# A float32 transformer step on one core: weight preparation in other steps, sample rows transposed later, one more Strassen pair in place of two plain gates

## The chip, the core and the metric

One core of a Trainium2 chip runs one launch. The metric is the device time in microseconds of that launch (us below). The engines of the core are named as in the profile: PE multiplies matrices (PEld is its weight load), DVE is the vector engine, ACT the activation engine, POOL the general engine, and SP issues the transfers (DMAs).

## The reference

One decoder layer over 1024 prompt rows and 8 x 4 sample rows, 1056 rows (tokens) in all, of width 1024, in float32:

```python
h = LN1(alpha*x + 0.5*SwiGLU_a(x))          # w1, w3: 1024x2816, w2: 2816x1024
z = h @ w_in + b_in                         # 42 column blocks of 128
A = dilated_window_attention(q, k, v of z)  # blocks 0..17
B = u * (tril(W_s) LN(v) + b)               # blocks 18..25 after gelu
h = LN2(alpha*h + (sigmoid(gA)*(A@w_oa) + sigmoid(gB)*(B@w_ob)) @ w_out)
y = LN3(alpha*h + 0.5*SwiGLU_b(h))          # gA: blocks 26..33, gB: blocks 34..41
```

It also returns the attention's key and value windows, for prompt and sample, and the normalised rows of the gating branch.

## The kernel before

**Arithmetic.** Every float32 operand is split in two (`split`, L252: a rounded high part copied by ACT, a low part subtracted by DVE), and every product is three matmuls of 128x128 by 128x264 (`mm3`, L238): high by high, high by low, low by high. The 1056 tokens are four chunks of C = 264. All matmuls of the weights stand on L242.

**Plain blocks and pairs.** A plain block of 128 output columns takes 8 row blocks x 3 matmuls in each of four chunks (`gate8`, L988, for the gates: 24 matmuls a chunk, evicted by ACT in L994 and sent to scratch). Two blocks together can go through a seven-product Strassen scheme (Winograd's form): the weights make seven combinations of halves (`prep`, L370), the activations make seven (`spread`, L329, in `self.T`), and each of the seven products takes 4 row blocks x 2 token halves x 3 matmuls (`product`, L416). The order is 1, 2, 6, 7, 5, 4, 3. `hidden` (L442) does so for one block of w1 beside one of w3, in both feed-forward parts (21 blocks in the first, 20 in the second), and `pair` (L1017) for two blocks of w_in. After each product come its evictions from the accumulators (L1034 on ACT, L1043 on DVE in a pair), traced in `urgent()`, and then a call of `between`. There are three sets of accumulator banks; the set `one` serves products 1, 6, 5 and 3, so a product waits until the evictions of the one before it in the same set are done.

**Preparation.** `prep` is a generator that `begin(f + 1)` starts at the head of block f and that `between` moves on by one step per product. In the kernel before its steps are: transfers of both weight blocks ab and cd (L376, L377) and the split of ab; the sums s12 (L386, L387); the split of s12 and half of s34 (L392); the rest of s34 (L394) and the split of cd's half; the split of s34. The sums run on POOL, or on DVE for the first pair and the first two feed-forward blocks. Two raw buffers (tag R), eight weight buffers (W) and two for the sums (Q) go round.

**Order.** The program is written in trace order, and a compiler pass with a simulated time line orders each engine's instructions; an engine then works strictly in that order. `urgent` raises the priority of evictions by 300. `fenced` (L154) makes what is traced inside it stand behind the last urgent instruction of DVE, of ACT, and behind the last weight transfer of SP. Background work stands in three queues, `bg`, `slow` and `mid`, and `tick(n, m)` takes n steps of `bg`, m of `slow`, 3 of `mid`, all fenced. `prep`'s steps are not fenced.

**The stage of w_in** (`widen`, L1087). Three gates are computed chunk by chunk behind the first layer norm; then three more (`NLEAD = 6`), each with its own weights in W. Their eight ticks take steps of `spread` too. During the last of them pair 0 is prepared. Then 13 pairs: nine of q, k and v, two each of v and u of the gating branch. After a pair of q, k and v, `sample_rows` (L1370) pauses for 4 steps of `bg` (three per product), then PE transposes the sample rows of the pair's two outputs (L1375). After every third such pair `sample` (L1388), the sample rows' attention, joins `slow`: it streams keys and values (kv) in 256 KB pieces that DVE multiplies and reduces (L1421, L1422, L1432, L1437). Behind the pairs `mix` does ten plain gates, the prompt's attention and the two output projections.

Of the kernel before, what the change touches and what calls it, by code (L numbers as in the profile page):

```python
# [16 lines left out]
ALU = mybir.AluOpType  # L17
# [13 lines left out]
FB = 2816 // P  # L31
# [28 lines left out]
REST = 3  # L60
GAP = 4
AFTER = 100
LATE = 16
MID = 3
HOP = (4, 1, 4)
# [3 lines left out]
FENCED = (mybir.EngineType.DVE, mybir.EngineType.Activation, mybir.EngineType.SP)  # L69
QKV = [s * 6 + 2 * g + hp for hp, g in HPG for s in range(3)]  # L70
GATES = [*range(34, 42), *range(26, 34)]
NLEAD = 6
NTAIL = 10
LAST = 3
EARLY = 6
BESIDE = {2: 13, 4: 14, 5: 15}
CHUNKED = 3
SPLIT = [*QKV, 22, 23, 24, 25, 18, 19, 20, 21, *GATES[NLEAD : 16 - NTAIL]]
DENSE = GATES[:NLEAD] + GATES[16 - NTAIL :]
# [4 lines left out]
class Trunk:  # L84
# [285 lines left out]
    def prep(self, src, f, H, engine):  # L370

        nc = self.nc
        lo, hi, n = slice(0, H), slice(H, 2 * H), 2 * H
        with self.tc.high_priority(offset=URGENT):
            ab, cd = self.R([P, D])[:, :n], self.R([P, D])[:, :n]
            nc.sync.dma_start(ab, src[1])  # L376
            dma = nc.sync.dma_start(cd, src[0])  # L377
        self.copy_state(dma, 2)
        tt = engine.tensor_tensor
        ah, al = self.W([P, D]), self.W([P, D])  # L380
        self.split(ah[:, :n], al[:, :n], ab)
        if f == LASTW2:
            h34, l34 = self.held([P, D], F32R), self.held([P, D], F32R)
        yield
        s12 = self.Q([P, D])
        tt(s12[:, lo], cd[:, lo], cd[:, hi], op=ALU.add)  # L386
        tt(s12[:, hi], s12[:, lo], ab[:, lo], op=ALU.subtract)  # L387
        yield
        s34 = self.Q([P, D])
        h12, l12 = self.W([P, D]), self.W([P, D])  # L390
        self.split(h12[:, :n], l12[:, :n], s12[:, :n])
        tt(s34[:, lo], ab[:, lo], cd[:, lo], op=ALU.subtract)  # L392
        yield
        tt(s34[:, hi], ab[:, hi], s12[:, hi], op=ALU.subtract)  # L394
        part = lambda h, l, o=0: [((h, l), o + k * P) for k in range(H // P)]
        if n == D:
            dd = self.S([P, D], F32R)
            self.split(dd[:, lo], dd[:, hi], cd[:, hi])
            p4 = part(dd[:, lo], dd[:, hi])
        else:  # L400
            p4 = []
            for h, l, w in ((ah, al, D - n), (h12, l12, H - (D - n))):
                o = H + len(p4) * P
                self.split(h[:, n : n + w], l[:, n : n + w], cd[:, o : o + w])
                p4 += part(h, l, n)[: w // P]
        yield
        if f != LASTW2:
            h34, l34 = self.S([P, D], F32R), self.S([P, D], F32R)
        self.split(h34[:, :n], l34[:, :n], s34[:, :n])
        self.L[f] = {  # L410
            1: part(ah, al), 2: part(ah, al, H), 5: part(h12, l12), 6: part(h12, l12, H),
            7: part(h34, l34), 3: part(h34, l34, H), 4: p4,
        }
        yield

    def product(self, t, p, f, first):  # L416
        while any(p not in t for t in self.T):
# [257 lines left out]
    def ffn(self, w13, w2p, w2, i, mode, resid):  # L675
        nc, preps = self.nc, {}
        plain = PLAIN[: 1 if i == 0 else 2]
        blocks = [f for f in range(FB) if f not in plain] + [FB + g for g in range(NG * (KB // 2))]
        after = dict(zip(blocks, blocks[1:]))

        def begin(f):
            if f < FB:
                preps[f] = self.prep(w13[f], f, KH * P, nc.gpsimd if f > 2 else nc.vector)
            else:
                preps[f] = self.prep(w2p[f - FB], f, HP, nc.vector)
            next(preps[f])

        if i == 0:
            self.lns = {}
            self.T, self.L = ({}, {}), {}  # L690
            units = self.lead_in(w13)
            self.new_x(1)
            self.consts()
            s0, s1 = (self.spread(j, self.Y, self.A, self.nc.vector) for j in range(2))
            begin(1)
            with self.tc.high_priority(offset=URGENT):
                for k in range(2):
                    self.load_x(self.nc.sync, 3, k, 0, KH)
            for c, work in enumerate((((2,), s0, s0, 1), ((3,), s0, 1, 1), (s1, s1, s1, 1), (1, s0))):
                self.hidden8(units, 0, c)  # L700
                for x in work:
                    if isinstance(x, tuple):
                        self.new_x(*x)
                    else:
                        next(preps[x] if x == 1 else x, None)
            self.bg.extend((s0, s1))
        else:
            lead, s1 = self.early
            lns, self.lns = self.lns, {}
            self.drain(lns[NC - 2])  # L710
            self.step(self.bg, 1)
            begin(1)
            for c in range(NC):
                self.drain(lns.pop(c))
                if c == NC - 1:
                    self.bg.append(s1)
                    self.step(self.bg, 2)
                for f, u in zip(plain, lead):
                    self.hidden8(u, f, c)
                    if c:  # L720
                        with self.chained():
                            next(preps[1], None)
            lead = self.early = None
        self.sqs = {}
        self.Y = self.A = None
        loads = deque(self.load_sums(resid))
        total = len(loads)

        def ready(f):
            for _ in preps.pop(f):  # L730
                pass
            if f in after:
                begin(after[f])

        def between(f, bg, slow=0):
            if after.get(f) in preps:
                next(preps[after[f]], None)
            self.tick(bg, slow)

        def load(n):  # L740

            with self.tc.high_priority(offset=URGENT):
                while loads and total - len(loads) < n:
                    loads.popleft()()

        for f in blocks[: FB - len(plain)]:
            ready(f)
            if f == FB - 1:
                load(2)
            count = iter(range(1, 8))  # L750

            def step():
                between(f, STEPS["strassen"])
                if f == FB - 1:
                    load(min(HEAD, 2 + 4 * next(count)))

            self.hidden(f, step)
            del self.L[f]
        self.T = ({}, {})
        self.normed = [None] * NC  # L760
        self.out(w2, i, mode, ready, between, load)
# [63 lines left out]
    def out(self, w2, i, mode, ready, between, load):  # L825
# [101 lines left out]
        for c in range(NC):  # L927
            early = 6 if c == 0 else 0
            if mode != "out":
                self.hold_normed(c)  # L930
                if c == 2:
                    self.early = [self.unit(self.a["wzp"][n], slot=True, ahead=AFTER) for n in range(CHUNKED)]
            for n in range(KB):
# [14 lines left out]
    def tables(self):  # L948
# [8 lines left out]
        for g in range(3):  # L957
            nc.sync.dma_start(oh[g], a["ohP"][:, g])
        yield from self.pause(LATE)
        for g in range(3):  # L960
# [126 lines left out]
    def widen(self):  # L1087
# [13 lines left out]
        preps = {}  # L1101
# [14 lines left out]
        units = Y = None  # L1116
        for n in range(CHUNKED, NLEAD):
            w = self.unit(a["wzp"][n])
            if n == NLEAD - 1:
                begin(0)  # L1120
            for c in (1, 3, 0, 2):
                self.gate8(w, DENSE[n], c, AF.Sigmoid, STEPS["lead"], 1)
                if n == NLEAD - 1:
                    next(preps[0], None)
        self.A = None
        for f in range(NZ):
            for _ in preps.pop(f):
                pass
            if f < NZ - 1:
                begin(f + 1)  # L1130

            def between():
                if f + 1 in preps:
                    next(preps[f + 1], None)
                self.tick(STEPS["strassen"], 1)

            self.pair(f, between)
            del self.L[f]
# [230 lines left out]

    def sample_rows(self, *blocks):  # L1370
        nc, a = self.nc, self.a
        yield from self.pause(4)
        p = self.ax_tile()[:NS, : 2 * P].rearrange("p (s x) -> p s x", s=2)
        for x, (_, t) in enumerate(blocks):
            nc.tensor.transpose(p[:, x], t[:, NP:], self.ident)  # L1375
        st = self.M([NS, 2, P])
        nc.vector.tensor_copy(st, p)
        for x, (nb, _) in enumerate(blocks):
            s, g, hp = nb // 6, (nb % 6) // 2, nb % 2
            L = GROUPS[g][0]  # L1380
            nc.sync.dma_start(
                self.sD[g, s, 2 * hp : 2 * hp + 2].rearrange("h t e -> t h e"),
                st[:, x].rearrange("t (h e) -> t h e", h=2),
            )
            if s:
                nc.sync.dma_start(a[f"ws{g}"][:, L - 4 :, 256 * (s - 1) + P * hp : 256 * (s - 1) + P * hp + P], st[:, x])
# [522 lines left out]
```

## Time and profile before

| | us |
|---|---|
| median of 3 runs | 2153.39 |
| lowest and highest of them | 2152.51, 2158.67 |
| the profiled execution | 2154.51 |
| its span, first to last instruction | 2152.5 |

In the profile's terms the stages are: the lead-in (0 to 40), the first w1/w3 stage (40 to 461), its w2 stage (to 655), the layer norm with the three chunked gates (to about 751), three plain gates (to 789), 13 pairs (to about 1059), `mix` with its layer norm (to about 1495), the second w1/w3 stage (to about 1904), its w2 stage and the last layer norm.

How to read the lines: a row of the windows gives for a stretch its length, each engine's busy us with the number of its instructions, the granted clock of PE as a share of full speed, the busy share of the transfer engines and their GB/s. A row of the timeline gives start, length, engine, line, operation, output<-input, shape and count of neighbours merged into it, and in brackets the idle time before it and what ended that. A row of the chain of waits gives start, length and what the chain went through.

### The profile page before, as it was taken

How to read it: one execution, taken by the hardware profiler on the slowest of the kernel's cores; microseconds unless marked ns; L12 is line 12 of the kernel's file. 1: busy time of each engine (PE TensorE's matmuls, PEld its weight loads, DVE VectorE, ACT ScalarE, POOL GpSimd, SP SyncE). 2: the span in 40 equal slices, each digit the busy share in tenths (PEclk: the TensorE clock that was granted, in tenths of full speed). 3: DMA queues.
4: the chain of work that ended last, by engine and by line, in shares of the span. 5: the costliest groups of instructions: out<-in, count | busy, mean ns of one | idle time of the engine just before them, and what ended most of it. 6: DMA issues, size and time to landing. Idle time of an engine off the chain costs nothing.

```text
span 2152.5 us, 43254 instructions
## 1 busy us (share of the span) xinstructions
PE 2122.6 (99%) x17307; PEld 2085.6 (97%) x17307; DVE 1549.5 (72%) x2727; ACT 889.4 (41%) x1680; POOL 317.1 (15%) x249
## 2 busy tenths in 40 slices
PE   9999999999999999999999999999999999999997
PEld 8999999999999999999988889999999999999997
DVE  8877767747789834777767758787667777657887
ACT  5444444422124634333476544164444444421224
POOL 0432322200000011323000000000323323100000
PEclk9999999999999999999999999999999999999998
DMA  4444555598885335676865765423454554596852
GB/s 155 145 140 170 183 166 168 189 338 315 327 325 176 130 103 177 201 231 198 296 211 187 223 190 177 154 110 110 144 174 156 183 173 153 194 408 267 311 186 81
DMA packets 168377, 426.51 MB, mean 198 GB/s; under 512 B 24352, under 2 KB 59792, under 8 KB 165488
## 3 DMA queue, kind: packets, MB, share of 16 engines
q1 hardware_dynamic: 167744, 423.21, 56.4%
q8 instruction: 135, 2.21, 0.4%
q10 hardware_dynamic: 432, 0.54, 0.1%
q14 instruction: 66, 0.54, 0.1%
HBM read 304.31 MB, written 165.57 MB: 218 GB/s over the span
## 4 chain that ended last, share of the span: by engine, by line
PE 89%; DVE 4%; DMA 4%; POOL 1%; issue 1%; ACT 0%; SPq 0%; ACTq 0%; DVEq 0%; POOLq 0%
PE ax L242 46%; PE mm L242 39%; DMA R<-wz 1%; PE ax L1206 1%; DMA M<-kv 1%; DMA S<-cD 1%; PE ax L1255 1%; PE ax L1232 1%; DVE W L254 1%; DMA S<-hD 0%; DVE S L632 0%; POOL Q L392 0%; POOL Q L387 0%; DVE S L254 0%; PE ax L621 0%
## 5 line engine op out<-in xcount | busy, mean ns | idle before, releaser
L242 PE MATMUL mm<-S,W 128*128 128x264 f32 x5400 | 713.6, 287 | 8.0 <-ACT S L253 2.3
L242 PE MATMUL ax<-S,W 128*128 128x264 f32 x5400 | 708.6, 285 | 1.3 <-ACT S L1034 1.1
L242 PEld LDWEIGHTS mm<-S,W 128*128 128x128 f32 x5400 | 677.1, 189 | 21.0 <-issue 7.0
L242 PEld LDWEIGHTS ax<-S,W 128*128 128x128 f32 x5400 | 678.5, 189 | 4.0 <-ACT S L1034 2.4
L242 PE MATMUL ax<-S,S 128*128 128x264 f32 x3240 | 475.9, 284 | 1.0 <-ACT S L1034 0.5
L242 PEld LDWEIGHTS ax<-S,S 128*128 128x128 f32 x3240 | 427.7, 188 | 1.7 <-DVE S L1043 0.9
L242 PE MATMUL mm<-S,S 128*128 128x264 f32 x2280 | 359.4, 286 | 2.6 <-DVE S L925 2.6
L242 PEld LDWEIGHTS mm<-S,S 128*128 128x128 f32 x2280 | 311.0, 189 | 3.9 <-issue 2.9
L253 ACT CAST W<-R 128x256 fp32r<-128x256 f32 (+2 forms) x175 | 130.6, 764 | 307.5 <-PE mm L242 139.9
L386 POOL TENSOR_TENSOR Q<-R 128x512 f32<-128x512 f32 x49 | 68.1, 1390 | 800.8 <-DMA R<-w13a 198.2
L254 DVE TENSOR_TENSOR W<-R,W 128x256 fp32r<-128x256 f32 (+2 forms) x175 | 154.6, 887 | 23.3 <-ACT W L253 21.7
L253 ACT CAST W<-Q 128x1024 fp32r<-128x1024 f32 (+1 forms) x78 | 76.8, 984 | 217.2 <-POOL Q L387 88.1
L820 DVE SCALAR_TENSOR_TENSOR S<-ax,S 128x264 f32<-128x264 f32 x240 | 99.7, 429 | 66.1 <-PE ax L242 65.7
L462 DVE TENSOR_TENSOR S<-ax,M 128x264 f32<-128x264 f32 x82 | 32.6, 433 | 144.7 <-PE ax L242 144.7
L254 DVE TENSOR_TENSOR S<-Q,S 128x1024 fp32r<-128x1024 f32 (+1 forms) x78 | 113.6, 1456 | 5.5 <-ACT S L253 5.4
L110 POOL CAST S<-ones 128x1 fp32r<-128x1 f32 x36 | 12.5, 355 | 675.7 <-PE ax L242 226.0
L254 DVE TENSOR_TENSOR W<-Q,W 128x1024 fp32r<-128x1024 f32 (+1 forms) x78 | 90.6, 1161 | 29.6 <-ACT W L253 29.6
L253 ACT CAST S<-Q 128x1024 fp32r<-128x1024 f32 (+1 forms) x78 | 76.7, 984 | 68.4 <-PE ax L242 49.8
L254 DVE TENSOR_TENSOR S<-S,M 128x528 fp32r<-128x528 f32 x72 | 84.6, 1175 | 2.5 <-ACT M L253 0.7
L253 ACT CAST S<-R 128x512 fp32r<-128x512 f32 (+1 forms) x62 | 42.0, 677 | 98.9 <-DMA sumsA<-S 40.6
L387 POOL TENSOR_TENSOR Q<-Q,R 128x512 f32<-128x512 f32 x49 | 81.0, 1653 | 2.7
L394 POOL TENSOR_TENSOR Q<-R,Q 128x512 f32<-128x512 f32 x49 | 79.7, 1627 | 1.2
(209 smaller groups left out, 2042.5 us busy)
## 6 DMA issues: line engine op xcount, KB each, us to landing
ws<-st SPq DMA_DIRECT2D x144, 256.0 KB
S<-sumsA SPq DMA_DIRECT2D x63, 528.0 KB
S<-sumsB SPq DMA_DIRECT2D x63, 528.0 KB
M<-kv SPq DMA_DIRECT2D x96, 256.0 KB
sumsA<-M SPq DMA_DIRECT2D x90, 264.0 KB
sumsB<-M SPq DMA_DIRECT2D x90, 264.0 KB
R<-w13b SPq DMA_DIRECT2D x44, 512.0 KB
R<-w13a SPq DMA_DIRECT2D x42, 512.0 KB
```

The lines of the kernel that those rows point to most:

```text
L110: self.nc.gpsimd.tensor_copy(t[:, 0, :1] if len(shape) == 3 else t[:, :1], self.ones[:, :1])
L242: mm = lambda a, b, s, e: nc.tensor.matmul(o, a[:, cc], b, start=s, stop=e, skip_group_check=True)
L253: a = self.nc.scalar.copy(hi, src)
L254: b = self.nc.vector.tensor_tensor(lo, src, hi.bitcast(F32), op=ALU.subtract)
L386: tt(s12[:, lo], cd[:, lo], cd[:, hi], op=ALU.add)
L387: tt(s12[:, hi], s12[:, lo], ab[:, lo], op=ALU.subtract)
L394: tt(s34[:, hi], ab[:, hi], s12[:, hi], op=ALU.subtract)
L462: go(one, 5, False, lambda x: tt(h[:, x, 1], one[x], p7[:, x], op=ALU.add))
L820: nc.vector.scalar_tensor_tensor(y(x, r, e), bank[x], HALF, y(x, r, e), op0=ALU.mult, op1=ALU.add)
L1206: m = nc.tensor.matmul(pS[h][:, r, :nk], q[e, i * P : (i + 1) * P], k[e, k0 : k0 + nk], start=True, stop=True)
L1232: nc.tensor.transpose(pT[r][:, h, o], s[:, r, h, o], self.ident)
L1255: nc.tensor.matmul(pv[0][e, (i % 4) * P : (i % 4 + 1) * P], V[:, i - (nb - 1) + b, e], sT[:, r, h, b * P : b * P + P], start=b == 0, stop= ...
```

## The change

1. `prep` for w1/w3 and for w_in (`f < FB`; the w2 blocks have higher numbers) has the same number of steps with other contents: transfers; split of ab and s12; half of s34; split of s12, the rest of s34 and the split of cd's half; split of s34. 
2. These steps go through the new `advance`, which fences them, but for the last w1/w3 block, the w2 blocks and pair 0.
3. `sample_rows` pauses for 8 steps in place of 4.
4. Gates 38 and 39 are no longer plain: `NLEAD` is 4, and they are a fourteenth pair, the last, with a sigmoid. Pair 0 is prepared during the one plain gate that is left, with one more call of its generator at that gate's last chunk.

```diff
+ROWS = 8
-NLEAD = 6
+NLEAD = 4
-BESIDE = {2: 13, 4: 14, 5: 15}
+BESIDE = {2: 11, 4: 12, 5: 13}
@@ prep
         tt = engine.tensor_tensor
+        late = f < FB
+        if late:
+            yield
         ah, al = self.W([P, D]), self.W([P, D])
         self.split(ah[:, :n], al[:, :n], ab)
         if f == LASTW2:
             h34, l34 = self.held([P, D], F32R), self.held([P, D], F32R)
-        yield
+        if not late:
+            yield
         s12 = self.Q([P, D])
         tt(s12[:, lo], cd[:, lo], cd[:, hi], op=ALU.add)
         tt(s12[:, hi], s12[:, lo], ab[:, lo], op=ALU.subtract)
         yield
         s34 = self.Q([P, D])
+        if late:
+            tt(s34[:, lo], ab[:, lo], cd[:, lo], op=ALU.subtract)
+            yield
         h12, l12 = self.W([P, D]), self.W([P, D])
         self.split(h12[:, :n], l12[:, :n], s12[:, :n])
-        tt(s34[:, lo], ab[:, lo], cd[:, lo], op=ALU.subtract)
-        yield
+        if not late:
+            tt(s34[:, lo], ab[:, lo], cd[:, lo], op=ALU.subtract)
+            yield
         tt(s34[:, hi], ab[:, hi], s12[:, hi], op=ALU.subtract)
...
+    def advance(self, gen, fenced=True):
+        if gen is not None:
+            with self.fenced() if fenced else ExitStack():
+                next(gen, None)
@@ ffn
         def between(f, bg, slow=0):
-            if after.get(f) in preps:
-                next(preps[after[f]], None)
+            self.advance(preps.get(after.get(f)), f < FB - 1)
             self.tick(bg, slow)
@@ widen
                 self.gate8(w, DENSE[n], c, AF.Sigmoid, STEPS["lead"], 1)
                 if n == NLEAD - 1:
-                    next(preps[0], None)
+                    for _ in range(2 if c == 2 else 1):
+                        next(preps[0], None)
...
             def between():
-                if f + 1 in preps:
-                    next(preps[f + 1], None)
+                self.advance(preps.get(f + 1))
                 self.tick(STEPS["strassen"], 1)
@@ sample_rows
-        yield from self.pause(4)
+        yield from self.pause(ROWS)
```

## The prediction

> **What bounds the kernel now.** I read the head of the page first, then the busy time by stage (windows), then the chain of waits, then the timelines of PE, ACT and DVE where the windows show PE short of work.
>
> ```profile
> span 2152.5 us, 43254 instructions
> PE 2122.6 (99%) x17307; PEld 2085.6 (97%) x17307; DVE 1549.5 (72%) x2727; ACT 889.4 (41%) x1680; POOL 317.1 (15%) x249
> ```
> ```profile
> 40.00:461.00 421.00, 421.00 (x3458) 421.00 (x3457) 304.49 (x411) 182.33 (x320) 119.87 (x76) 1.00 0.51 170
> ...
> 655.00:790.00 135.00, 132.13 (x1067) 131.18 (x1066) 94.96 (x142) 73.73 (x125) 7.26 (x8) 0.99 0.37 125
> 790.00:893.00 103.00, 103.00 (x849) 102.70 (x847) 59.02 (x94) 40.55 (x79) 27.42 (x20) 1.00 0.52 175
> 893.00:1003.00 110.00, 106.69 (x850) 104.55 (x849) 84.09 (x148) 43.17 (x86) 29.94 (x20) 0.98 0.66 214
> 1003.00:1058.00 55.00, 54.48 (x448) 54.27 (x447) 40.09 (x71) 23.43 (x44) 5.72 (x4) 1.00 0.74 250
> ...
> 1095.00:1300.00 205.00, 200.40 (x1692) 179.98 (x1691) 134.15 (x402) 119.59 (x319) 4.13 (x11) 1.00 0.60 193
> ...
> 1495.00:1904.00 409.00, 409.00 (x3366) 409.00 (x3365) 285.92 (x400) 172.74 (x305) 111.22 (x72) 1.00 0.52 180
> ```
>
> The first figures of a row are its length and PE's busy time. PE sets the time: 99% of the span. In both w1/w3 stages it has no idle time at all (421.00 of 421, 409.00 of 409), so an easier preparation has nothing to give there. Of the pairs, the stretch from 893 to 1003 stands out: 850 matmuls in 110 us, where 790 to 893 did 849 in 103. Only two things can therefore shorten this kernel by this edit: fewer matmuls, and that stretch.
>
> **Part 1, the work (a fourteenth pair for two gates).** Two gates are 2 x 4 chunks x 24 = 192 matmuls; a pair is 7 products x 24 = 168.
>
> ```profile
> 734.17 1.61 PE L242 MATMUL ax<-S,W 128*128 128x264 f32 x12
> ...
> 751.45 37.96 PE L242 MATMUL mm<-S,W 128*128 128x264 f32 x312
> ...
> 789.25 3.09 PE L242 MATMUL ax<-S,W 128*128 128x264 f32 x24
> ```
> ```profile
> 800.94 5.96 PE ax L242 x49
> ...
> 883.59 5.96 PE ax L242 x49
> ...
> 1014.50 5.93 PE ax L242 x49
> ...
> 1034.88 5.96 PE ax L242 x49
> ```
>
> The first three rows are PE's timeline (the first is used in part 3): 312 matmuls from 751.45 to 789.25, that is 37.80 / 312 = 0.1212 us each, so two gates are 192 x 0.1212 = 23.26 us. The other four are the chain at the same product of four pairs. A pair without sample rows, which the gate pair is, takes 1034.88 - 1014.50 = 20.38 us. The sum of part 1 is 23.26 - 20.38 = 2.9 us saved.
>
> **Part 2, the stretch 893 to 1003.** The same rows measure its loss. Four pairs from 800.94 to 883.59 take 82.65, or 20.66 each with their sample rows; the six from 883.59 to 1014.50 take 130.91, against 6 x 20.66 = 123.96. So 6.95 us are lost. Where?
>
> ```profile
> 913.96 0.39 PE L1375 MATMUL ax<-ident,S 128*32 128x128 f32 x2 [0.53 <-ACT S L1034]
> 914.59 3.44 PE L242 MATMUL ax<-S,W 128*128 128x264 f32 x24 [0.23 <-ACT S L1034]
> ...
> 927.61 3.60 PE L242 MATMUL ax<-S,S 128*128 128x264 f32 x24 [0.38 <-DVE S L1043]
> ...
> 933.46 3.07 PE L242 MATMUL mm<-S,W 128*128 128x264 f32 x24
> 937.75 0.40 PE L1375 MATMUL ax<-ident,S 128*32 128x128 f32 x2 [1.21 <-ACT S L1034]
> 938.38 4.98 PE L242 MATMUL ax<-S,W 128*128 128x264 f32 x24 [0.23 <-ACT S L1034]
> ...
> 1002.68 3.20 PE L242 MATMUL ax<-S,W 128*128 128x264 f32 x24 [0.58 <-ACT S L1034]
> ```
> ```profile
> 911.75 1.05 ACT L253 CAST W<-Q 128x1024 fp32r<-128x1024 f32 x1 [4.89 <-POOL Q L387]
> 912.71 1.20 ACT L1034 ACTIVATE S<-ax,cols 128x264 f32<-128x264 f32 x3
> ...
> 935.26 1.05 ACT L253 CAST W<-Q 128x1024 fp32r<-128x1024 f32 x1 [13.15 <-POOL Q L387]
> 936.22 1.47 ACT L1034 ACTIVATE S<-ax,qb 128x256 f32<-128x256 f32 x5
> ...
> 1000.46 1.05 ACT L253 CAST W<-Q 128x1024 fp32r<-128x1024 f32 x1 [5.55 <-POOL Q L387]
> 1001.41 1.59 ACT L1034 ACTIVATE S<-ax,cols 128x264 f32<-128x264 f32 x4
> ```
> ```profile
> 940.00:945.00 5.00, 5.00 (x31) 5.00 (x31) 3.19 (x7) 3.16 (x5) 0.00 (x0) 0.70 0.68 227
> ```
>
> PE's five waits on ACT add up to 0.53 + 0.23 + 1.21 + 0.23 + 0.58 = 2.78 us. Behind them 24 matmuls took 3.44, 4.98 and 3.20 in place of 3.09 (row at 789.25): 0.35 + 1.89 + 0.11 = 2.35 more. The 1.89 are the clock: 940 to 945 has a granted clock of 0.70. That makes 5.1 us. The wait on DVE costs 0.38 + (3.60 - 3.09) = 0.9, and 0.9 stay unexplained.
>
> ACT's timeline names the cause. Each time ACT stood in its order at the split of s12 (L253, W<-Q), waiting for POOL, and the evictions that PE needed (L1034) were queued right behind it. The transposes of the sample rows (L1375) wait for the last of those evictions.
>
> The change takes exactly this away. The split of s12 moves from the step after product 2 to the step after product 6, and, fenced, it must stand behind that product's evictions. In the case at 935.26 product 2 was over at 936.5 (row at 933.46), product 6 would have been at 939.5, and POOL's sums were done at 935.26: ACT would not have waited. The transposes also move one product later (8 pauses at 3 per product, against 4), another 2.9 us for the evictions. What is late next on ACT is the split of ab, now behind product 1's evictions, which waits for a transfer; the eviction behind it is product 6's, two products later, so it has 5.8 us. So I take all 5.1 as saved, and leave the DVE wait and the rest. The ends: nothing saved, if another instruction blocks ACT or DVE as long; 6.95 at most.
>
> A rule of the Trainium skill (TensorE: Matmul & The Clock Gate, section "HAM oscillation — how this bites in real kernels") is that PE should have "no PE-idle gaps >~3.4µs", or its clock is cut. The gaps ahead of the cut here were 1.21 and 0.23 us, so by that rule the cut would not be theirs and would stay, and the whole sum would be 1.9 us smaller; the trace has it right behind them, so I count it with them.
>
> **Part 3, what is added or loses cover.**
>
> *Pair 0 comes 23.26 us earlier.* Gate 3 ends at 751.45 + 96 x 0.1212 = 763.1, and pair 0 starts there.
>
> ```profile
> 758.98 1.26 DVE L348 TENSOR_TENSOR S<-S,S 128x1056 fp32r<-128x1056 f32 x1 [1.65 <-ACT S L343]
> ...
> 764.23 1.23 DVE L254 TENSOR_TENSOR W<-Q,W 128x1024 fp32r<-128x1024 f32 x1 [2.26 <-ACT W L253]
> ```
> ```profile
> 769.18 1.29 POOL L394 TENSOR_TENSOR Q<-R,Q 128x512 f32<-128x512 f32 x1
> ```
>
> The spread's last combination was done at 760.2, in six steps at one per tick; the ticks left ahead of pair 0 are three of the chunked gates and four of gate 3, so it still fits. Pair 0's s12 was split at 764.23 to 765.4, when gate 3 gave its weight buffers back; with two gates' weights fewer in the eight buffers it need not wait for that, and even then it stands 0.6 us ahead of product 6 at 766.0. Pair 1's sums ended at 770.5, and pair 1 starts at about 763.1 + 20.4 - 2.9 (half of product 1 of pair 0 ran ahead as filler at 734.17, and the rest soon after) = 780.6. I take 0. If the cover fails, pair 0 waits some 2 us, and another 1.9 for a clock cut.
>
> *Other edits.* The gate pair adds one change of ACT's function table, 1.28 us by the row below, against the 2.9 us of a product that lies between an eviction and the reuse of its bank: 0. Sample steps: 77 ticks of `slow` run in the pairs where 70 did, which takes seven steps from `mix`; its stretch 1095 to 1300 has 205 - 200.40 = 4.6 us of PE idle, of which I count none, with ends of 1 us either way.
>
> ```profile
> 1026.15 1.28 ACT L1057 ACT_TABLE_LOAD   x1
> ```
>
> *The w1/w3 stages.* 41 blocks get the same fences. PE is never idle there, so the price is zero unless a fence makes the weights late; that is the slower rival.
>
> **Sum.** 2.9 + 5.1 = 8.0 us. On the profiled execution the span goes from 2152.5 to 2144.5, and its 2154.51 to 2146.5. That execution is 1.1 above the median, so for the median I take 2153.39 - 8.0 = 2145.4, which is 0.37% less. A difference under 0.3%, 6.5 us, is about what a measurement of this kernel can't tell from none; the limits are 2146.9 and 2159.9.
>
> **The rivals.**
>
> *A new wait takes the old one's place.* DVE also stands in order, behind the sample's pieces:
>
> ```profile
> L1421 DVE TENSOR_TENSOR M<-M,X 128x512 f32<-128x512 f32 (+1 forms) x34 | 29.0, 869 | 13.2 <-DMA M<-kv 13.2
> L1432 DVE TENSOR_TENSOR M<-M,X 128x512 f32<-128x512 f32 (+1 forms) x28 | 21.7, 788 | 16.7 <-DMA M<-kv 14.9 <-DMA M<-sD 0.9 <-ACT X L1427 0.9
> ```
>
> DVE spends 13.2 + 14.9 us of the pairs waiting for kv, and splits and evictions stand behind those waits. If the fenced low-part subtractions come later for it, the next weights do too, and PE waits for DVE as long as it did for ACT. For it: the wait at 927.61. Against: only one of six was DVE's. Then only part 1 is left: 2150.5.
>
> *The clock cut stays* (it falls where the clock's own window falls, whatever the gap, and so may fall again): 2153.39 - (8.0 - 1.9) = 2147.3. Against it stands that 940 to 945 is the only cut between 790 and 1003 and follows the longest gap there. This is what the rule of the Trainium skill named above (TensorE: Matmul & The Clock Gate) would make of it.
>
> *More is saved*, all 6.95 of the stretch and the 0.5 us by which PE's busy time falls short in 1003 to 1058: 2.9 + 7.5 = 10.4, so 2143.0.
>
> *Slower: the fence in the w1/w3 blocks.* The split of ab now stands behind product 1 on ACT and ahead of product 6's eviction. It waits for the transfer of ab:
>
> ```profile
> 166.78 0.33 SPq L376 DMA_DIRECT2D R<-w13a  x1
> ```
> ```profile
> 902.53 4.80 DMA R<-wz
> ```
> ```profile
> 177.24 3.10 PE L242 MATMUL ax<-S,W 128*128 128x264 f32 x24
> ```
>
> Issued at 166.78 and 4.80 us on the way (a pair's transfer of the same size), ab is there at 171.6; the next block's product 1 ends at 180.2. The margin is 8.6 us. It decides only if the raw buffer comes free that much later; then each block's weights are late, and at 0.25 us a block, 41 blocks lose 10.3: 2153.4 - 2.9 + 10.3 = 2160.8.
>
> *The edit does nothing to the order* (the pass had put these instructions there anyway) falls together with the first rival: 2150.5.
>
> **Chances.** Forecast 0.52 (own range 2143.0 to 2148.5), new wait or no effect 0.22, clock cut stays 0.08, more saved 0.11, slower 0.07. Below 2146.9 lie about 0.36 of the forecast's 0.52 and the 0.11: faster 0.47. Within 0.3%: the other 0.16, 0.22 and 0.08: 0.46. Slower: 0.07. The range 2142.0 to 2153.5 leaves out the slower rival, and the outer ends of the others: a transition that loses 2 to 4 us, or a `mix` that gains 1.
>
> **What would show it.**
>
> ```profile
> L253 ACT CAST W<-Q 128x1024 fp32r<-128x1024 f32 x13 | 13.7, 1051 | 82.7 <-POOL Q L387 79.2 <-PE mm L242 3.5
> ```
>
> Right: 24 fewer matmuls on L242; PE's waits on ACT L1034 between the gates and the last pair gone (2.78 us before), ACT's split of W<-Q with little idle before it (82.7 us for 13 of them before, most of it harmless), clock 1.00 through the pairs, and 14 pairs within 14 x 20.6 us; both w1/w3 stages as long as before. Wrong: PE waits on DVE L1043 or on W L254 in the pairs; PE short of work at the first pair; PE idle above zero in the w1/w3 stages; or a stretch of half clock elsewhere, at 1.9 us each.

## The result, and the profile after

The changed kernel takes 2150.45 us (median of 22 runs, 2147.52 to 2156.13), the kernel before 2154.91 us (22 runs, 2151.29 to 2158.67). The ratio is 0.998, with a 95% interval of 0.9974 to 0.9986: 0.2% faster, 4.5 us between the medians. That is clear of noise, and a little over half of the 8.0 us that were forecast. The profiled execution took 2147.6 us, 2.85 under the median of its kernel, while the one of before lay within 0.4 of its own median; so the two profiles together flatter the change, and a second profile of each is used below.

The head of the page after, and the stages by the windows:

```profile
span 2145.8 us, 42827 instructions
...
PE 2113.6 (98%) x17283; PEld 2080.6 (97%) x17283; DVE 1536.5 (72%) x2735; ACT 888.7 (41%) x1689; POOL 292.1 (14%) x253
```
```profile
766.00:880.00 114.00, 114.00 (x942) 113.87 (x941) 69.54 (x112) 46.10 (x88) 32.55 (x25) 1.00 0.56 190
880.00:1003.80 123.80, 123.80 (x1022) 123.70 (x1021) 106.16 (x172) 53.86 (x105) 35.79 (x25) 1.00 0.70 233
1003.80:1048.66 44.86, 44.86 (x372) 44.86 (x371) 35.74 (x66) 20.77 (x36) 4.78 (x4) 1.00 0.76 253
...
1085.00:1290.00 205.00, 195.72 (x1664) 177.27 (x1664) 125.29 (x378) 119.97 (x313) 3.34 (x11) 1.00 0.58 180
...
1487.00:1896.00 409.00, 409.00 (x3368) 409.00 (x3368) 273.98 (x400) 169.75 (x308) 97.65 (x72) 1.00 0.52 177
```

The page shows 24 matmuls fewer (17283 for 17307). In the pairs PE is busy for every microsecond and the clock is whole, where 893 to 1003 had 3.3 us of idle time and a clock of 0.98. But 205 us of `mix` now hold 9.3 us of PE idle (205 - 195.72), where before they held 4.6: the gain is partly given back behind the pairs. The chain at the same product of two pairs, and ACT's group for the split of s12 in the stage of w_in, show the cure itself:

```profile
777.20 6.21 PE ax L243 x51
...
1003.82 6.19 PE ax L243 x51
```
```profile
L254 ACT CAST W<-Q 128x1024 fp32r<-128x1024 f32 x13 | 13.8, 1060 | 0.0
```

Eleven pairs take 1003.82 - 777.20 = 226.62, or 20.60 each, and the split (L254 now) has 0.0 us of idle time ahead of it, where it had 82.7. The waits of PE that grew behind the pairs show what came in its place:

```profile
PE mm L243 <- DVE S L1598: 4.1, 6, 1.6
...
PE ax L1219 <- DVE X L1229: 2.0, 2, 1.5
...
PE ax L1202 <- DMA S<-zD: 1.2, 1, 1.2
```
```profile
PE mm L242 <- DVE S L1585: 1.9, 3, 1.3
...
PE ax L1206 <- DVE X L1216: 0.5, 1, 0.5
```

The first fence is after, the second before (the columns are the sum, the number and the longest). All are in `mix`: L1598 (L1585 before) evicts the two products with w_oa and w_ob, called the output product below, and L1229 (L1216) reduces the attention's scores.

To compare stages between programs, four marks are read from each trace: the last eviction ahead of the gates' stage (L925 before) and that of the leading gates (L994), the last eviction of the pairs (L1034), and the last of the output product (L1585). The "end" column runs from the last eviction of the second w2 stage (L820) to the last of the plain w2 blocks behind it (L925).

| profile | leading gates | pairs | mix to the last of L1585 | end | ratio to before (95%) |
|---|---|---|---|---|---|
| before | 73.9 | 274.8 (13) | 280.9 | 50.6 | |
| before again (b1) | 73.9 | 271.2 (13) | 283.6 | 50.5 | 1.0001 (0.9991 to 1.0011) |
| after | 50.8 | 285.8 (14) | 286.6 | 52.0 | 0.998 (0.9974 to 0.9986) |
| after again (a1) | 50.7 | 285.8 (14) | 287.9 | 52.0 | 0.9976 (0.9966 to 0.9985) |
| part 1 alone (p1) | 50.5 | 299.3 (14) | 288.4 | 50.9 | 1.0019 (1.001 to 1.0027) |
| part 2 alone (p2) | 73.0 | 266.8 (13) | 282.1 | 52.0 | 0.9978 (0.9969 to 0.9987) |
| m1, 7 steps held | 50.7 | 285.8 (14) | 284.1 | 52.1 | 0.9959 (0.9945 to 0.9973) |
| m2, gate pair first | 50.7 | 287.0 (14) | 283.4 | 52.0 | 0.9976 (0.9965 to 0.9987) |
| m3, column sums later | 50.7 | 285.8 (14) | 289.7 | 52.0 | 0.9987 (0.9979 to 0.9996) |
| m4, p2 with 7 steps more | 73.0 | 267.0 (13) | 290.0 | 51.9 | 1.0021 (1.0011 to 1.0031) |
| q1, m1 without fences | 50.5 | 293.0 (14) | 283.4 | 51.0 | 0.9978 (0.9968 to 0.9988) |
| q2, m1 with the old steps | 51.5 | 291.1 (14) | 284.1 | 51.5 | 0.998 (0.997 to 0.999) |
| q3, m1, rows after 4 | 50.7 | 285.9 (14) | 284.1 | 52.1 | 0.9963 (0.995 to 0.9975) |
| q4, m1, old w1/w3 | 50.8 | 286.1 (14) | 283.7 | 51.0 | 0.995 (0.9936 to 0.9963) |
| r1, q4 catching up | 50.8 | 286.1 (14) | 288.4 | 50.8 | 0.9968 (0.9956 to 0.998) |
| r2, q4 held late | 50.8 | 286.1 (14) | 287.6 | 51.2 | 0.9963 (0.995 to 0.9975) |
| r3, q4 holding 14 | 50.8 | 286.1 (14) | 298.7 | 51.1 | 1.0012 (1.0003 to 1.002) |
| r4, q4 with 13 pairs | 73.0 | 266.8 (13) | 285.0 | 50.6 | 0.9959 (0.9946 to 0.9971) |

The expectations below give `mix` up to an earlier mark, the 24th instruction on that line with the waits in DVE's queue counted, which is the 21st eviction in some programs and the 22nd in others. Their figures are 50.3 to 51.1 us under this column's for the same profile, and 62.9 for r3.

Two profiles of the kernel before differ by 3.6 us in the pairs and by 2.7 in `mix`, so one profile of it gives neither to better than that. Some of the `mix` times also hold stretches of half clock: one of 3.4 us in a1, p1, m1, m2, m4, q3, r1 and r2, three in m3, one of 10.2 us in r3, and none in the other eight. One costs at most about 1.9 us, by the prediction's row at 938.38. The profile after has none, and its 286.6 still stands 3.0 and 5.7 above the two of before.

### The profile page after: what moved, and what is told of

It reads as the page before. It is cut to its first block, busy times and chain, and to the rows that moved or that the text cites. A ratio compares the mean times of both kernels' runs of the same rounds, so it can differ in the third digit from the quotient of the medians.

```text
span 2145.8 us, 42827 instructions
## 1 busy us (share of the span) xinstructions
PE 2113.6 (98%) x17283; PEld 2080.6 (97%) x17283; DVE 1536.5 (72%) x2735; ACT 888.7 (41%) x1689; POOL 292.1 (14%) x253
## 4 chain that ended last, share of the span: by engine, by line
PE 90%; DMA 5%; DVE 3%; issue 1%; ACT 1%; SPq 0%; ACTq 0%; POOL 0%; DVEq 0%
PE ax L243 48%; PE mm L243 38%; PE ax L1219 1%; DMA S<-cD 1%; DMA S<-sumsB 1%; PE ax L1268 1%; PE ax L1245 1%; DMA S<-hD 1%; DMA S<-zD 1%; DMA sumsB<-M 0%; DVE S L646 0%; DMA partA<-M 0%; DMA R<-w2pb 0%; PE mm L1564 0%; DVE S L569 0%
## 5 line engine op out<-in xcount | busy, mean ns | idle before, releaser
L243 PE MATMUL ax<-S,W 128*128 128x264 f32 x5472 | 717.3, 285 | 0.1
L243 PE MATMUL mm<-S,W 128*128 128x264 f32 x5232 | 692.0, 287 | 13.6 <-DVE S L1598 4.1
L243 PEld LDWEIGHTS mm<-S,W 128*128 128x128 f32 x5232 | 656.6, 189 | 24.9 <-DVE S L1598 6.0
L255 DVE TENSOR_TENSOR W<-R,W 128x1024 fp32r<-128x1024 f32 (+3 forms) x174 | 151.4, 872 | 108.2 <-ACT W L254 105.3
L254 ACT CAST W<-R 128x1024 fp32r<-128x1024 f32 (+3 forms) x174 | 129.8, 763 | 213.0 <-PE mm L243 67.8
L255 DVE TENSOR_TENSOR S<-Q,S 128x1024 fp32r<-128x1024 f32 (+1 forms) x79 | 90.2, 1142 | 49.4 <-ACT S L254 49.3
L254 ACT CAST W<-Q 128x1024 fp32r<-128x1024 f32 (+1 forms) x79 | 78.1, 988 | 101.1 <-DVE Q L392 93.8
L480 ACT ACTIVATE S<-S 128x528 f32<-128x528 f32 x82 | 48.6, 638 | 154.1 <-DVE S L479 154.1
L481 DVE TENSOR_TENSOR S<-S,M 128x264 f32<-128x264 f32 x82 | 95.0, 1186 | 14.5 <-ACT S L480 13.6
L254 ACT CAST S<-Q 128x1024 fp32r<-128x1024 f32 (+1 forms) x79 | 78.0, 988 | 24.3 <-DVE Q L403 15.0
L472 ACT COPY M<-ax 128x264 f32<-128x264 f32 x82 | 28.7, 380 | 135.9 <-issue 85.1
L474 ACT COPY M<-ax 128x264 f32<-128x264 f32 x82 | 30.4, 379 | 127.9 <-PE ax L243 127.9
L1047 ACT ACTIVATE S<-ax,cols 128x264 f32<-128x264 f32 (+5 forms) x99 | 40.4, 495 | 86.3 <-PE ax L243 81.8
```

Of the source, the lines that this page charges most:

```text
L243: mm = lambda a, b, s, e: nc.tensor.matmul(o, a[:, cc], b, start=s, stop=e, skip_group_check=True)
L254: a = self.nc.scalar.copy(hi, src)
L255: b = self.nc.vector.tensor_tensor(lo, src, hi.bitcast(F32), op=ALU.subtract)
L472: go(one, 1, True, lambda x: copy(r1[:, x], one[x]))
L474: go(one, 6, False, lambda x: copy(u2[:, x], one[x]))
L480: lambda x: nc.scalar.activation(h[:, x], h[:, x], AF.Silu),
```

## The experiments

**Both kernels again (a1, b1).** No edit.

> The changed kernel again, for a second profile of the same program. Theory A (the stalls moved): the pairs again run at 20.6 us each without a wait of PE, and the stages behind them again give back 2 to 4 us of the 10 that the trace shows at the last pair; 4 to 5 us faster than the kernel before. Theory B (the clock): the first profile was a lucky one with a single half-clock stretch between 10 and 2090 us; this one has two or three, at 1.7 us each, in other places, and a span of 2148 to 2150. Theory C (the fences cost time in the w1/w3 stages): 20.50 us a block against 20.47 of before again, about 1 us over both stages.

> The kernel before again, for a second profile and as the measure of noise: ratio 1.000 within 0.1%. Theory A: the waits on ACT in the pairs and the half-clock stretch at 940 come back, since the order of ACT's instructions is the cause, and the pairs' stretch again loses 6 to 8 us. Theory B: the half-clock stretch comes at another place or not at all.

The stages of the changed kernel repeat within 1.3 us, and `mix` is as slow as in the first profile (287.9); so the loss behind the pairs belongs to the program, as theory A says. The kernel before has its waits on ACT in the pairs again, and again a stretch of reduced clock behind the longest:

```profile
PE ax L242 <- ACT S L1034: 2.2, 2, 2.0
PE ax L1375 <- ACT S L1034: 0.5, 1, 0.5
```
```profile
995.00:1000.00 5.00, 2.98 (x20) 2.77 (x19) 4.12 (x7) 2.54 (x5) 2.17 (x2) 0.87 0.50 147
1000.00:1005.00 5.00, 5.00 (x35) 5.00 (x35) 2.33 (x3) 3.89 (x7) 0.00 (x0) 0.79 0.62 223
```

It stands at 1000 and not at 940, and the pairs take 271.2 us, 3.6 less than in the first profile. So theory A was wrong on the place, which theory B had right, and its 6 to 8 us of loss are here about 4.4 (271.2 against the 266.8 of p2 below). The waits on ACT came back, and a1 has none in the pairs and no cut of the clock there. So theory B falls in the main point, that the whole effect is luck with the clock. Theory C's 0.3 us per w1/w3 stage stays open until q4.

**The parts alone (p1, p2).** p1 is the kernel before with

```diff
-NLEAD = 6
+NLEAD = 4
-BESIDE = {2: 13, 4: 14, 5: 15}
+BESIDE = {2: 11, 4: 12, 5: 13}
```

and p2 the changed kernel with these two lines taken back.

> Part 1 alone: fourteen pairs and four leading gates, preparation and sample rows as before. By the sum of the prediction 2.9 us faster than before (ratio 0.9987) with the waits on ACT in the pairs still there. Theory A: less than that, 1 to 2 us, if the shorter cover ahead of pair 0 or the stage behind the pairs takes some back. Theory B: 2.9 less the noise of the cuts.

> Part 2 alone: thirteen pairs and six leading gates as before, with the preparation in its new steps, fenced, and the sample rows transposed later. By the sum of the prediction 5.1 us faster (ratio 0.9976), with no wait of PE on ACT in the pairs. Theory A: the pairs gain 6 to 7 us and the stages behind them give 2 to 4 back, so 3 us net. Theory B: only the idle time of 2.8 us. Theory C: 1 us less than either.

p1 went the other way than every theory had it: 0.19% slower, where 24 fewer matmuls should have made it faster. Its leading gates give the 23.4 us back (50.5 for 73.9), but its `mix` takes 288.4 against 282.3 (the mean of before and b1), and its pairs 299.3 against 273.0 + 20.4, with more waits than before:

```profile
PE ax L242 <- ACT S L1034: 4.3, 6, 2.7
PE ax L1375 <- ACT S L1034: 1.7, 3, 0.9
```

p2 carries the whole gain of the change, and its `mix` is untouched at 282.1. So what slows `mix` comes with part 1. The first suspect is the slow queue, which has seven ticks more ahead of `mix`; another is that gates 38 and 39 are written later (theory A2).

**Seven steps of the slow queue (m1, m2, m3, m4).** m1 takes no slow step during the fourteenth pair; m2 puts the gate pair ahead of the others; m3 leaves the steps and puts seven empty ones ahead of the column sums; m4 is p2 with seven steps more, two for one in each call of the last pair.

```diff
 m1: -                self.tick(STEPS["strassen"], 1)
     +                self.tick(STEPS["strassen"], int(f < NZ - 1))
 m2: -SPLIT = [*QKV, 22, 23, 24, 25, 18, 19, 20, 21, *GATES[NLEAD : 16 - NTAIL]]
     +SPLIT = [*GATES[NLEAD : 16 - NTAIL], *QKV, 22, 23, 24, 25, 18, 19, 20, 21]
     -            if f % 3 == 2:
     -                self.slow.append(self.sample(f // 3))
     +            if f % 3 == 0:
     +                self.slow.append(self.sample(f // 3 - 1))
 m3: +            yield from self.pause(7)
 m4: -                self.tick(STEPS["strassen"], 1)
     +                self.tick(STEPS["strassen"], 1 + (f == NZ - 1))
```

> The changed kernel with no step of the slow queue during the fourteenth pair, so that mix begins with the sample rows' attention where it stood in the kernel before (70 steps done, not 77). Theory A1 (the seven steps that mix no longer has cost it about 5 us): from the last pair to the 24th eviction of the first output product it takes 231 to 233 us as before, not 236 to 237, and the time is 4 to 5 us under the changed kernel's (ratio to before 0.9955 to 0.996). Theory A2 (mix loses for another reason, such as the later gates 38 and 39, or the order that the pass finds): 236 to 237 us and 0.998 again.

> The changed kernel with the pair of gates ahead of the nine pairs of q, k and v, not last; the sample rows' attention again has 70 steps in the pairs. Theory A1: mix takes 231 to 233 us and the ratio is 0.9955 to 0.996, as with the held steps. Theory A2: if the late writing of gates 38 and 39 is what costs mix, the same; if it is the pass's order, about 0.998.

> The changed kernel with seven empty steps ahead of the column sums of w_out, which follow the sample rows' attention in the slow queue and would otherwise begin seven steps earlier than before. Theory A1a (the steps cost mix because the column sums' loads and reductions come early and meet the attention's end): mix takes 231 to 233 us, ratio 0.9955 to 0.996. Theory A1b (it is the missing steps of the sample attention themselves): 236 to 237 us, ratio 0.998.

> Thirteen pairs and six leading gates with the new preparation, and two steps of the slow queue in place of one in each of the last pair's seven calls: mix begins seven steps further, without the fourteenth pair. Theory A1: mix takes 236 to 237 us, not the 231.5 of the same kernel without the extra steps, and the ratio goes from 0.998 to about 1.000. Theory A2: it stays at 231.5 us and 0.998.

Theory A1 holds in both directions. Held back, the steps give `mix` 284.1 and 283.4 us, a cut of the clock included in each; brought forward in thirteen pairs, with no gate moved at all, they raise it from 282.1 to 290.0 and turn p2's 0.9978 into 1.0021. The waits of m4 are those of the changed kernel, only longer:

```profile
PE mm L243 <- DVE S L1598: 4.7, 6, 2.1
...
PE ax L1219 <- DVE X L1229: 3.3, 3, 2.4
```

Seven empty steps ahead of the column sums do not bring the time back (m3: 0.9987), so theory A1a falls. m3's `mix` of 289.7 holds three such cuts of the clock, some 5 us, so it does not tell whether they cured a part. m2 is a partial miss: its `mix` came back as expected, but its ratio is 0.9976, not 0.996. Its pairs took 1.2 us more, and the rest of that difference is not explained.

**What in part 2 does it (q1, q2, q3, q4).** All four start from m1.

```diff
 q1: -            with self.fenced() if fenced else ExitStack():
     +            with ExitStack():
 q2: -        late = f < FB
     +        late = False
 q3: -ROWS = 8
     +ROWS = 4
 q4: -    def prep(self, src, f, H, engine):
     +    def prep(self, src, f, H, engine, late=False):
     -        late = f < FB
     -            self.advance(preps.get(after.get(f)), f < FB - 1)
     +            self.advance(preps.get(after.get(f)), False)
     -            preps[f] = self.prep(a["wz7"][f], f, KH * P, nc.gpsimd if f else nc.vector)
     +            preps[f] = self.prep(a["wz7"][f], f, KH * P, nc.gpsimd if f else nc.vector, True)
```

> The kernel with the held steps (ratio 0.9959, 285.8 us in the fourteen pairs), but no step of the preparation fenced; its new steps and the later transposes stay. Theory D1 (the split of s12 stands ahead of the evictions only because it is traced too early, so the new steps alone cure it): 285 to 287 us in the pairs, no wait of PE on ACT there, ratio 0.996. Theory D2 (the fence does it, since the pass may put any step ahead of an eviction by its simulated times): 290 to 293 us, waits on ACT again, ratio 0.998 to 0.999.

> The kernel with the held steps, with the preparation's steps as they were, but fenced; the later transposes stay. Theory D1: the split of s12 again comes after product 2 and ACT stands at it for POOL; 290 to 293 us in the pairs, ratio 0.998 to 0.999. Theory D2: 285 to 287 us and 0.996.

> The kernel with the held steps, with the sample rows transposed after 4 steps as before. Theory E1 (the transposes waited only because ACT was late): 285 to 287 us in the pairs, no change. Theory E2 (they need the later place): 0.5 to 2 us more, with waits of PE on ACT at the transposes.

> The kernel with the held steps, with the preparation of w1 and w3 as before, steps and fences; only w_in's is new. Theory C (the edit costs time in the feed-forward parts): both w1/w3 stages 0.3 us shorter (368.5 and 389.9 us between the marks as before, not 368.8 and 390.3), the last w2 and layer norm stretch back from 52.0 to 50.6, so 1 to 2 us faster than the held kernel, ratio 0.995. Against it: no change, 0.996, if that stretch came from elsewhere.

Neither edit as it stands in q1 and q2 cures the pairs alone. Without fences (q1) they take 293.0, and ACT stands at the split of s12 for POOL as long as ever (93.2 us); with fences and the old steps (q2) they take 291.1. The fences nearly end the wait at that split (6.1 us), but PE still waits for ACT's evictions and now once for DVE's (the first fence is q1, the second q2: PE's waits in the pairs; the third and fourth ACT's groups of q1 and q2):

```profile
PE ax L243 <- ACT S L1047: 4.2, 4, 1.6
```
```profile
PE ax L243 <- ACT S L1047: 2.0, 2, 1.0
PE mm L243 <- ACT S L1047: 0.9, 1, 0.9
PE ax L243 <- DVE S L1056: 0.9, 1, 0.9
```
```profile
L254 ACT CAST W<-Q 128x1024 fp32r<-128x1024 f32 x13 | 13.7, 1051 | 93.2 <-POOL Q L392 93.2
```
```profile
L254 ACT CAST W<-Q 128x1024 fp32r<-128x1024 f32 x13 | 13.7, 1052 | 6.1 <-POOL Q L392 6.1
```

What held ACT in q2 is another split. These are its rows and PE's ahead of the longest wait:

```profile
936.38 1.05 ACT L254 CAST W<-R 128x1024 fp32r<-128x1024 f32 x1 [7.03 <-DMA R<-wz]
937.33 0.85 ACT L1047 ACTIVATE S<-ax,cols 128x264 f32<-128x264 f32 x2
...
937.86 3.19 PE L243 MATMUL ax<-S,W 128*128 128x264 f32 x24 [1.04 <-ACT S L1047]
```

It is the split of ab (W<-R), which waited 7.03 us for its transfer, with the evictions right behind it. `begin` takes the first step of `prep` without a fence, and in the old steps that first step holds the split of ab. So q2 left one blocking split unfenced. Its time is the one that theory D1 gave, its cause is not; whether the old steps would do with all of them fenced was not run. What q1 shows is that the new steps need the fences, as theory D2 has it.

The later transposes do nothing (q3: 285.9 and 0.9963, as m1; theory E1). Taking w1 and w3 out of the edit helps as theory C has it: the end goes from 52.1 to 51.0 (50.6 was expected), and the ratio from 0.9959 to 0.995. These two intervals overlap, so the time alone does not show it; the marks do, since the end is 51.9 to 52.1 in all seven programs with new steps and fences in w1 and w3 (the changed kernel, p2, m1 to m4, q3) and 50.5 to 51.5 in all others.

q4 beats both kernels: 2144.82 us against 2155.08 of before on the same chip, 0.5% (0.37 to 0.64%).

**Where the seven steps cost (r1 to r4).** All start from q4. r1 takes two slow steps in the first seven calls of the tail gates, so that the sample attention ends early again; r2 has no hold in the pairs but holds seven steps in the last calls of the tail gates (the plain gates of `mix`); r3 holds two pairs; r4 goes back to thirteen pairs with one slow step in every call.

```diff
 r1: +        more = iter(range(7))
     -                    self.tick(STEPS["tail"], 1)
     +                    self.tick(STEPS["tail"], 1 + (next(more, None) is not None))
 r2: -                self.tick(STEPS["strassen"], int(f < NZ - 1))
     +                self.tick(STEPS["strassen"], 1)
     -                    gate(n, c, STEPS["tail"], 1)
     +                    gate(n, c, STEPS["tail"], int(c == 0 and n < NLEAD + NTAIL - 1))
 r3: -                self.tick(STEPS["strassen"], int(f < NZ - 1))
     +                self.tick(STEPS["strassen"], int(f < NZ - 2))
```

> The best kernel so far (steps held in the fourteenth pair, preparation of w1 and w3 as before; ratio 0.995, mix 233.4 us to the 24th eviction of the output product), with two slow steps in place of one in the first seven calls of the tail gates, so that the sample rows' attention again ends early in mix. Theory F1 (what costs is that it ends inside the tail gates): mix 236 to 239 us, ratio 0.9965 to 0.9975. Theory F2 (what counts is where it stands when mix begins): 233 us, 0.995.

> The best kernel with the slow steps of the fourteenth pair given back (77 steps ahead of mix, as in the changed kernel), and seven slow steps held in the last nine calls of the tail gates, so that the sample rows' attention ends late, in the output product. Theory F1: mix 232 to 234 us, ratio 0.995. Theory F2: mix 236 to 237 us, ratio 0.9965 to 0.9975.

> The best kernel with the slow steps held in the last two pairs (63 ahead of mix). Theory F1: no more than 1 us better or worse, since the sample rows' attention ends in the output product in both; 2 to 4 us worse if its last steps come to stand ahead of that product's evictions. Theory F2: another 3 to 5 us faster, ratio 0.993.

> The best kernel with thirteen pairs and six leading gates and one slow step in every call, so that the sample rows' attention stands at 70 steps as well. By the count of matmuls it is 2.9 us slower than the best kernel (ratio 0.9964 against 0.995). If the fourteenth pair's saving is eaten by the shorter cover ahead of pair 0, it is equal.

r1 goes as F1 has it: caught up at the head of `mix`, the steps cost as much as if they had run in the pairs (288.4, 0.9968), so where the queue stands when `mix` begins is not what counts, and F2 falls. (The ratios' intervals overlap with q4's; the marks and waits show it.) But r2 does not save F1: with the end held late, `mix` still takes 287.6. Its waits are others than r1's:

```profile
PE ax L1218 <- DVE X L1228: 4.3, 3, 2.1
PE mm L243 <- DVE S L1597: 1.3, 3, 0.6
```

```profile
PE mm L243 <- DVE S L1597: 5.1, 6, 1.9
PE ax L1218 <- DVE X L1228: 2.2, 1, 2.2
```

The first fence is r2, the second r1. In r2 the output product's evictions are well again (1.3 us, against 5.1), but PE waits for the attention's score reductions (4.3 us). That the sample's steps, early on DVE, stand in their way there is argued, not shown. r3 shows the other edge; held by fourteen, the sample attention is not done when the output product needs its rows, and PE waits for DVE ahead of their transposition (L1483). Its half clock of 10.2 us follows that wait. At 1.0012 it is some 13 us above q4, where theory F1 gave 4 at most:

```profile
PE ax L1483 <- DVE X L1480: 6.7, 1, 6.7
PE mm L243 <- DVE S L1597: 5.3, 6, 2.3
```

r4 is 0.9959 beside q4's 0.995. The difference, 1.9 us, has the sign of the 2.9 us that the matmuls give, with intervals that overlap.

One thing goes with the loss in all eighteen profiles: where in `mix` the sample attention's pass over the keys ends (DVE multiplying the pieces by the query). The last start on these lines (after, then before) less the last eviction of the pairs, 1048.7 and 1062.2, is 67.5 us after and 86.2 before:

```profile
L1434 DVE TENSOR_TENSOR M<-M,X x51: 419/686/1779, 828.0 to 1116.2; 128x512 f32<-128x512 f32 x48, 128x256 f32<-128x256 f32 x3
...
L1421 DVE TENSOR_TENSOR M<-M,X x51: 402/687/1786, 853.8 to 1148.4; 128x512 f32<-128x512 f32 x48, 128x256 f32<-128x256 f32 x3
```

It is 67 to 73 us in the seven profiles whose `mix` takes 286.6 to 290.0 (both of after, p1, m3, m4, r1, r2), 85 to 88 in the ten with 280.9 to 285.0, and 136 in r3. r2, whose values end even later than before (210 us behind the pairs), loses with its early keys. Why this place matters was not tested.

## Why the forecast was half right

The forecast was 8.0 us with an own range of 2143.0 to 2148.5; the median of 2150.45 lies outside that range, though inside the wider one, 2142.0 to 2153.5. Two terms came out, two that were put at nothing did not.

*Part 1, the work: right.* The leading gates fell by 23.1 us and a pair without sample rows takes 20.4, which leaves 2.7; 2.9 was the sum. Nothing is lost at pair 0: PE's timeline after runs on from gate 3 (first row) without a gap.

```profile
751.05 11.80 PE L243 MATMUL mm<-S,W 128*128 128x264 f32 x96
762.69 0.28 PE L243 MATMUL ax<-S,W 128*128 128x264 f32 x1
762.81 3.08 PE L243 MATMUL mm<-S,W 128*128 128x264 f32 x24
765.72 3.06 PE L243 MATMUL ax<-S,W 128*128 128x264 f32 x24
```

*Part 2, the pairs: the mechanism right, the term too small.* The split of s12 was what ACT stood at, and steps and fences together removed it. 5.1 was forecast. Over two profiles each, the pairs went from 273.0 to 285.8, of which 20.4 are the fourteenth: 7.6 saved (9.4 against the first profile of before, 5.8 against the second). No wait of PE on another engine is left in the pairs, so the wait on DVE went too. The later transposes, which the prediction counted as part of the cure, did nothing (q3).

*"Which takes seven steps from `mix` ... of which I count none, with ends of 1 us either way": this is the step that failed.* `mix` lost 5.0 us (282.3 to 287.3, two profiles each), five times the end that I gave it, and on the side on which I had expected a gain if anything. I read 4.6 us of idle time in `mix` as what there was to win, and took it that work which leaves a stretch can only ease it. But taking seven steps off the queue moves all that is left in it forward: the sample attention's last multiplication by the values (L1445, L1432 before) starts 154 us behind the last pair, not 204. DVE's sample work came into a stretch that was busier already. The windows show that, first the changed kernel, then the kernel before, at about the same distance behind the last pair (1048.7 and 1062.2):

```profile
1129.00:1169.00 40.00, 40.00 (x340) 35.19 (x339) 33.76 (x99) 24.84 (x74) 0.00 (x0) 1.00 0.60 186
...
1209.00:1229.00 20.00, 18.53 (x157) 16.44 (x156) 4.81 (x29) 13.91 (x45) 0.18 (x1) 1.00 0.42 146
```
```profile
1140.00:1180.00 40.00, 40.00 (x342) 35.42 (x341) 27.19 (x82) 24.30 (x70) 0.00 (x0) 1.00 0.56 180
...
1220.00:1240.00 20.00, 20.00 (x156) 16.32 (x155) 10.20 (x50) 12.83 (x48) 0.18 (x1) 1.00 0.51 178
```

DVE (third figure) rises from 27.19 to 33.76 us in the first and falls from 10.20 to 4.81 in the second. The sample attention's multiplications and reductions (L1434, L1435, L1445, L1450; L1421, L1422, L1432, L1437 before) account for all of the rise, 12.7 us against 4.2, and for half of the fall, none against 2.9. The second, 160 to 180 us behind the last pair, now has PE idle for 1.5 us. That the steps' place costs this is shown (m1, m4, r1). Which instruction of which step delays the attention and the output product is only argued: the pass lays out everything anew each time, and r2 shows that two different waits change places.

*"The price is zero unless a fence makes the weights late": also wrong, by about 1.5 us.* PE is never idle in the second w1/w3 stage after either (409.00 of 409). The first is 0.2 us longer between two evictions of product 1 (368.7 for 368.5) and 0.4 shorter between the first and last of product 3 (400.6 for 401.0), so no price shows there. It falls in the end (52.0 for 50.6), where nothing of the edit stands. q4 ties it to the edit of w1 and w3. PE's wait for the last w2 blocks' evictions (L938, L925 before) makes up 0.8 of it, 1.2 us for 0.4. It is 1.2 or 1.3 in every program that fences w1 and w3, q2 with its old steps among them, and 0.4 in all others; the rest is open.

The ledger of the spans, two profiles each: -2.7 for the work, -7.6 in the pairs, +5.0 in `mix`, +1.5 at the end and -0.4 elsewhere make -4.2, close to the 4.5 between the medians.

*The rivals.* None came true by its mechanism. The first, a new wait, gave 2150.5, almost the measured median, but that is luck: it had the pairs save nothing, where they saved more than forecast, and the new waits came some 140 us behind them. The clock: no profile without the ACT waits has a stretch of reduced clock in its pairs (thirteen profiles), and three of the five with them do (before, b1, p1). That bears out counting the 1.9 us with the gaps, though a gap does not always bring a cut: q1 waited 1.6 us at a time and has none there. In `mix` it is the same: a1 has a cut behind a gap of 2.2 us, the profile after has none behind one of 1.95. The rule of the Trainium skill (TensorE: Matmul & The Clock Gate, section "HAM oscillation — how this bites in real kernels") that only gaps above about 3.4 us matter is not borne out: the longest wait of b1 was 2.0 us.

## What to carry to other kernels

When a pass orders the instructions, look at what an in-order engine stands at ahead of the evictions that PE waits for; then move that work later in the trace and fence it. Without the fences the later steps did not cure it here (293.0 us against 285.8), and one split left outside the fences (q2) stood in the way again. Work in a background queue is not free because it is off the critical path: count how many of its steps fall before each stage, and hold that count when the number of calls that drive it changes. An edit that saves matmuls should be timed alone as well as with its companions: here it alone made the kernel slower, and with its companions and one line that kept the queue in step the whole was 0.4% faster (m1).

## What the runs showed of the hardware

A gap of PE of 1.2 to 2.7 us (before 1.2, b1 2.0, p1 2.7) can be followed by about 3.4 us at half clock: 939 to 944 of the kernel before has a granted clock of 0.66. It cost 1.9 us more where it could be read (24 matmuls in 4.98 us for 3.09). Where PE never waits its pace is so even that a stage repeats within 0.1 us across programs that prepare its weights alike. The fourteen pairs took 285.8 or 285.9 us in five profiles, and 286.1 in the four with the old w1/w3; the first w1/w3 stage took 368.5 or 368.7 in all eighteen. So such a stage's length in one profile tells more here than the median of 5 to 22 runs, whose range is 2 to 9 us.
